# Decoder trunk on one core: the block sums of the seven-product groups on GpSimd instead of VectorE

## The chip, the cores and the metric

The kernel runs on one core of one Trainium2 chip. The metric is the device time of one execution in microseconds, the median of several runs. The core has five engines that work side by side, each through its own queue in order: TensorE (PE in the profile, with PEld for its weight loads) multiplies matrices into PSUM; VectorE (DVE), ScalarE (ACT) and GpSimd (POOL) work elementwise; SyncE (SP) issues nearly all transfers between HBM and SBUF. Semaphores make one engine wait for another.

## The reference, cut to what matters

Two layers, each of three parts with a residual stream `h` of 512 tokens by 1024 features in float32: a feed-forward sub-layer, a mixing sub-layer (three kinds of attention, gated and merged), and a second feed-forward sub-layer.

```
def _swiglu(t, w_gate, w_up, w_down):
    return (jax.nn.silu(t @ w_gate) * (t @ w_up)) @ w_down
...
for l in range(DEPTH):
    f = _swiglu(_rmsnorm(h, ffn1_pre_g[l]), ffn1_w_gate[l], ffn1_w_up[l], ffn1_w_down[l])
    h = h + 0.5 * _rmsnorm(f, ffn1_post_g[l])
    ...
    h = h + _rmsnorm(merged @ w_out[l], mix_post_g[l])
    f = _swiglu(_rmsnorm(h, ffn2_pre_g[l]), ffn2_w_gate[l], ffn2_w_up[l], ffn2_w_down[l])
    h = h + 0.5 * _rmsnorm(f, ffn2_post_g[l])
```

The hidden width of the feed-forward sub-layers is 2816, that is 22 blocks of 128. There are four such sub-layers in all. In the profile their tiles carry the letters `a` (first of a layer) and `c` (second of a layer); `g`, `u` and `d` stand for the gate, up and down weights.

## The kernel before

**Two halves for every operand.** A float32 operand is written as the sum of a high and a low part in a format that TensorE multiplies at full rate. `split` (L179 to L193) makes both: ScalarE casts the high part (L182, `wh_` tiles for weights), VectorE subtracts it from the source (L183, `wl_`; with a scale L185 and L186). A product is then three matmuls (`mm3`, L204 to L208): high by high (L206), high by low (L207), low by high (L208).

**Seven products for eight.** Of the 22 hidden blocks, 16 are computed in two groups of 8 with seven block products in place of eight. Each operand is cut into two by two blocks, and the seven factors are blocks or sums of blocks. On the side of the activations the sums are formed by `sums` (L701 to L733, tiles `x..` and `u..`) and, for the down weights, by `first_factor` (L840 to L858, tiles `as`, `ah`, `al`), all on VectorE. On the side of the weights they are formed by `BlockUnit.load`.

**A weight block.** A `BlockUnit` (L275 to L332) stands for 256 rows by 512 columns of one block, as a tile of 128 partitions by 1024 columns. `fetch` (L301) issues its transfer from SyncE's queue: the block of product `n` goes into a `raw` tile, and for product 2 a second block goes into a kept tile `t` (`tg`, `tu` or `bt` in the profile). `load` (L319) forms what product `n` needs and splits it:

- product 2: `t = t - raw`
- product 3: `t = raw - t`
- product 5: `raw = t - raw`
- product 6: `t = raw - t`
- products 0, 1 and 4: `raw` as it is

These subtractions are line L328. The products come in the order 0, 2, 1, 3, 4, 5, 6, with two units in each; product 2 uses the `raw` tile of product 0 again, product 4 that of product 3. With two groups each of gate, up and down weights there are 8 x 6 = 48 sums in each feed-forward sub-layer, 192 in the kernel. The chain of one block is: transfer, sum where there is one, cast on ScalarE, low part on VectorE, 12 matmuls on TensorE.

**Buffers.** High and low weight tiles have four buffers each, `raw` tiles two, with further room in the `o` tiles while they are free (`BUFS` L102, `RINGS` L349). A block can so be cast at most three units ahead of TensorE, and a transfer starts when a `raw` tile is given back.

**What sets the order.** A queue of jobs (`Queue`, L351 to L462) is walked while the program is written down: each job loads its units, then those of the next jobs (`load_ahead`), then yields its matmuls; `PLAN` (L1668 to L1674) says in which order gate, up and down products of a sub-layer follow one another. The framework then orders each engine's instructions by when it expects their inputs and buffers. `tc.keep_in_program_order` pins an instruction behind what was written down before it on its engine. L329 and L330 pin a sum while the queue is `pinned`, which is so for the units loaded ahead at L646 to L648, and for product 2 of the down weights (`behind`, L907 and L908).

**GpSimd before.** It forms the identity and some constants, issues three small transfers (L122, L123, L156), clears tiles (L1126, L1167, L1217, L1322), and copies rows for the attention (L1215, L1216, L1326, L1390, L1392).

Of the kernel before, what the change touches and what calls it, by code (L numbers as in the profile page):

```python
# [14 lines left out]
ALU = mybir.AluOpType  # L15
# [8 lines left out]
def kernel(  # L24
# [38 lines left out]
    nc = tc.nc  # L63
# [169 lines left out]
    class Unit:  # L233
# [19 lines left out]
        def load(self):  # L253
            if self.h is not None:
                return
            self.fetch()
            self.split_from(self.raw[:])
            self.loaded()
# [16 lines left out]
    class BlockUnit(Unit):  # L275
# [43 lines left out]
        def load(self):  # L319
            if self.h is not None:  # L320
                return
            self.fetch()
            src = raw = self.raw[:]
            if self.n in (2, 3, 5, 6):
                t = self.keep.get(self.k0)
                src = raw if self.n == 5 else t
                a, b = (t, raw) if self.n in (2, 5) else (raw, t)
                ins = nc.vector.tensor_tensor(src, a, b, ALU.subtract)  # L328
                if Q.pinned or self.behind:  # L329
                    tc.keep_in_program_order(ins)  # L330
            self.cast = self.split_from(src)[0]
            self.loaded()  # L332

# [130 lines left out]
    Q = Queue()  # L464
# [1264 lines left out]
```

## Time and profile before

| | us |
|---|---|
| median of 3 runs | 2351.46 (2351.38 to 2351.54) |
| span of the profiled execution | 2349.9 |
| TensorE busy | 2337.9 (99%) |
| VectorE busy | 1799.9 (77%) |
| ScalarE busy | 1506.5 (64%) |
| GpSimd busy | 75.5 (3%) |
| VectorE busy on the sums of L328 | 234.0 (192 instructions) |
| mean DMA rate | 151 GB/s |

The profile comes from one execution, whose span is 1.6 us under the median. Its views give, for a group of instructions with the same line, engine and tiles, the busy time, the mean duration of one, and the idle time of the engine before them with what ended it. The table of stretches gives busy time in a part of the span. In the timeline each row is one instruction, or several alike in a row: start in us, duration in us, engine, line, operation, tiles written and read, shapes, and in brackets the idle time before it and what ended that. Matmuls overlap one another in TensorE, so that their rows are longer than their distance.

### The profile page before, as it was taken

What the parts mean: (1) busy time and instruction counts of PE and PEld (TensorE: products, weight loads), DVE (VectorE), ACT (ScalarE), POOL (GpSimd) and SP (SyncE); (2) the same over time, 40 slices, a digit from 0 to 9 for tenths busy, and PEclk for the clock granted to TensorE, in tenths of its full rate; (3) what the DMA queues carried; (4) which work ended last, traced back from release to release, by engine and by line L of the source; (5) the groups of instructions that cost most, each with busy time, mean ns of one, the idle gap of its engine ahead of it and who ended that gap; (6) DMA issues with size and microseconds to landing.
All of it is one profiled execution on the core that took longest, in us unless ns stands there. A gap on an engine that the chain in (4) does not pass through costs nothing.

```text
span 2349.9 us, 30935 instructions
## 1 busy us (share of the span) xinstructions
PE 2337.9 (99%) x11623; PEld 1977.6 (84%) x11623; DVE 1799.9 (77%) x2359; ACT 1506.5 (64%) x2302; POOL 75.5 (3%) x134
## 2 busy tenths in 40 slices
PE   9999999999999999999999999999999999999998
PEld 7888888888888888888898888888888888888887
DVE  8877877577777688878798788766677766888785
ACT  6677465576766556775656775655777665567744
POOL 0000000000111000000000000000001100000000
PEclk9999999999999999999999999999999999999999
DMA  6667454223323554774646665532323235556744
GB/s 206 186 180 220 149 197 127 81 83 88 90 72 107 189 188 152 198 197 152 226 144 184 204 175 185 182 108 72 100 72 99 73 123 190 171 182 182 217 142 147
DMA packets 297849, 354.96 MB, mean 151 GB/s; under 512 B 78282, under 2 KB 189154, under 8 KB 297700
## 3 DMA queue, kind: packets, MB, share of 16 engines
q1 hardware_dynamic: 297604, 352.97, 49.0%
q8 instruction: 91, 1.49, 0.3%
q14 instruction: 58, 0.48, 0.1%
q0 software_dynamic: 96, 0.03, 0.0%
HBM read 319.39 MB, written 16.78 MB: 143 GB/s over the span
## 4 chain that ended last, share of the span: by engine, by line
PE 89%; DVE 3%; DMA 3%; ACT 3%; issue 2%; SPq 0%; DVEq 0%; ACTq 0%
PE pg L207 3%; PE pg L206 3%; PE pg L208 3%; PE pda L207 3%; PE pdc L207 3%; PE pda L206 3%; PE pda L208 3%; PE pdc L208 3%; PE pdc L206 3%; PE pq L207 1%; PE pq L206 1%; PE pk L207 1%; PE pb L208 1%; PE pk L208 1%; PE pq L208 1%
## 5 line engine op out<-in xcount | busy, mean ns | idle before, releaser
L206 PE MATMUL pg<-us_a,wh_wg 128*128 128x512 f32 x384 | 150.9, 393 | 0.0
L207 PE MATMUL pg<-us_a,wh_wg 128*128 128x512 f32 x384 | 149.7, 390 | 0.0
L208 PE MATMUL pg<-us_a,wl_wg 128*128 128x512 f32 x384 | 149.7, 390 | 0.0
L183 DVE TENSOR_TENSOR wl_da<-raw_da,wh_da 128x1024 fp32r<-128x1024 f32 x50 | 61.0, 1224 | 44.3 <-ACT wh_da L182 44.2
L183 DVE TENSOR_TENSOR wl_dc<-raw_dc,wh_dc 128x1024 fp32r<-128x1024 f32 x50 | 61.0, 1224 | 42.3 <-ACT wh_dc L182 42.3
L207 PE MATMUL pdc<-wl_dc,ahc 128*128 128x512 f32 x224 | 87.7, 391 | 0.0
L207 PE MATMUL pda<-wl_da,aha 128*128 128x512 f32 x224 | 87.6, 391 | 0.0
L208 PE MATMUL pdc<-wh_dc,alc 128*128 128x512 f32 x224 | 87.2, 389 | 0.0
L208 PE MATMUL pda<-wh_da,ala 128*128 128x512 f32 x224 | 87.2, 389 | 0.0
L206 PE MATMUL pdc<-wh_dc,ahc 128*128 128x512 f32 x224 | 86.5, 389 | 0.0
L206 PE MATMUL pda<-wh_da,aha 128*128 128x512 f32 x224 | 86.5, 389 | 0.0
L208 PEld LDWEIGHTS pg<-us_a,wl_wg 128*128 128x128 f32 x384 | 72.1, 188 | 15.1
L207 PEld LDWEIGHTS pg<-us_a,wh_wg 128*128 128x128 f32 x384 | 72.2, 188 | 14.1
L206 PEld LDWEIGHTS pg<-us_a,wh_wg 128*128 128x128 f32 x384 | 72.1, 188 | 14.1
L182 ACT CAST wh_da<-raw_da 128x1024 fp32r<-128x1024 f32 x50 | 52.3, 1051 | 45.6 <-PE pda L208 14.3
L182 ACT CAST wh_dc<-raw_dc 128x1024 fp32r<-128x1024 f32 x50 | 52.3, 1049 | 43.0 <-PE pdc L208 14.1
L186 DVE SCALAR_TENSOR_TENSOR wl_wg<-raw_wg,wh_wg 128x1024 fp32r<-128x1024 f32 x48 | 58.4, 1221 | 21.6 <-ACT wh_wg L185 21.6
L201 DVE SCALAR_TENSOR_TENSOR ga<-pg,bgate,ga 128x512 f32<-128x512 f32 x48 | 35.9, 748 | 48.4 <-ACT ga L200 48.4
L182 ACT CAST wh_uc<-raw_uc 128x1024 fp32r<-128x1024 f32 x44 | 46.3, 1053 | 38.4 <-PE pwc0g L208 9.1
L182 ACT CAST wh_ua<-raw_ua 128x1024 fp32r<-128x1024 f32 x44 | 46.2, 1053 | 31.7 <-PE pwa1g L208 8.6
L185 ACT ACTIVATE wh_wg<-raw_wg 128x1024 fp32r<-128x1024 f32 x48 | 50.6, 1057 | 24.5 <-PE pv L1119 11.7
L183 DVE TENSOR_TENSOR wl_uc<-raw_uc,wh_uc 128x1024 fp32r<-128x1024 f32 x44 | 53.8, 1222 | 16.2 <-ACT wh_uc L182 16.0
(643 smaller groups left out, 8015.9 us busy)
## 6 DMA issues: line engine op xcount, KB each, us to landing
raw_da<-in_ffn_w_down_dram SPq DMA_DIRECT2D x66, 512.0 KB, 4.8
raw_dc<-in_ffn_w_down_dram SPq DMA_DIRECT2D x66, 512.0 KB, 4.3
raw_ga<-in_ffn_w_gate_dram SPq DMA_DIRECT2D x52, 512.0 KB, 4.5
raw_ua<-in_ffn_w_up_dram SPq DMA_DIRECT2D x52, 512.0 KB, 4.5
raw_gc<-in_ffn_w_gate_dram SPq DMA_DIRECT2D x52, 512.0 KB, 4.2
raw_uc<-in_ffn_w_up_dram SPq DMA_DIRECT2D x52, 512.0 KB, 4.0
raw_wg<-in_w_gate_dram SPq DMA_DIRECT2D x48, 512.0 KB, 3.6
raw_wo<-in_w_out_dram SPq DMA_DIRECT2D x24, 512.0 KB, 3.4
```

Source lines behind the costliest of these rows:

```text
L182: both = [nc.scalar.copy(h_ap, src)]
L183: make = lambda: nc.vector.tensor_tensor(l_ap, src, h_ap.bitcast(F32), ALU.subtract)
L185: both = [nc.scalar.activation(h_ap, src, AF.Copy, scale=scale)]
L186: make = lambda: nc.vector.scalar_tensor_tensor(l_ap, src, scale, h_ap.bitcast(F32), ALU.mult, ALU.subtract)
L201: nc.vector.scalar_tensor_tensor(t, z, minus, t, ALU.max, ALU.add)
L206: nc.tensor.matmul(pt, lh, rh, start=start, stop=False, skip_group_check=free)
L207: nc.tensor.matmul(pt, lh, rl, start=False, stop=False, skip_group_check=free)
L208: nc.tensor.matmul(pt, ll, rh, start=False, stop=stop, skip_group_check=free)
```

## The change

The subtraction of L328 is issued on GpSimd in place of VectorE, for every block sum and with the same operands and tiles. The pin of L329 and L330 goes, and nothing pins the sums on GpSimd. Casts, low parts, transfers, buffers and the order of the jobs in the program text stay as they are.

```
@@ -325,9 +325,7 @@
                 t = self.keep.get(self.k0)
                 src = raw if self.n == 5 else t
                 a, b = (t, raw) if self.n in (2, 5) else (raw, t)
-                ins = nc.vector.tensor_tensor(src, a, b, ALU.subtract)
-                if Q.pinned or self.behind:
-                    tc.keep_in_program_order(ins)
+                nc.gpsimd.tensor_tensor(src, a, b, ALU.subtract)
             self.cast = self.split_from(src)[0]
             self.loaded()
```

More of the change, by code (lines that the diff above doesn't have):

```diff
@@ L327, in load @@
                 a, b = (t, raw) if self.n in (2, 5) else (raw, t)
-                ins = nc.vector.tensor_tensor(src, a, b, ALU.subtract)
-                if Q.pinned or self.behind:
-                    tc.keep_in_program_order(ins)
+                nc.gpsimd.tensor_tensor(src, a, b, ALU.subtract)
             self.cast = self.split_from(src)[0]
```

## The prediction

> **What bounds the kernel now.** I read the page first, then the busy time by stretches, then the sums' own line, then pairs of instructions of VectorE and GpSimd that overlap.
>
> ```profile
> span 2349.9 us, 30935 instructions
> PE 2337.9 (99%) x11623; PEld 1977.6 (84%) x11623; DVE 1799.9 (77%) x2359; ACT 1506.5 (64%) x2302; POOL 75.5 (3%) x134
> ```
>
> TensorE (PE) is busy for all but 12.0 us of the span (a stall too short to leave a gap between two matmul rows isn't in this). Where the 12 us lie is in a table of stretches (length, then for PE, weight loads, VectorE, ScalarE and GpSimd the busy us and the number of instructions, then the granted clock, the DMA share and GB/s):
>
> ```profile
> 0.00:30.00 30.00, 27.39 (x162) 21.42 (x163) 19.67 (x46) 18.88 (x34) 3.15 (x9) 1.00 0.89 308
> 30.00:130.00 100.00, 99.56 (x476) 83.53 (x475) 89.37 (x88) 68.58 (x80) 0.00 (x0) 1.00 0.56 160
> ...
> 2210.00:2350.00 140.00, 133.02 (x586) 109.35 (x584) 102.01 (x111) 69.28 (x96) 0.00 (x0) 0.99 0.46 155
> ```
>
> The first 30 us and the last 140 us hold 2.6 + 7.0 = 9.6 of the 12.0 us, before the first sum and mostly behind the last one. Some 2.4 us of visible PE idling is left in the other 2180 us. So nothing that lightens another engine can win more than about 2.4 us, 0.1%. A change can only lose here, by making a weight block late. A measurement of this kernel can tell about 0.2% (4.7 us) from no change.
>
> The edited line is L328. The next fence holds its count and busy time on VectorE over the whole span, then one of its 18 groups by tile (ns min/median/max), then the largest entry of who waited for it (us, times):
>
> ```profile
> 0.00:2350.00 2350.00, 234.00 (x192) 1.00 0.49 151
> L328 DVE TENSOR_TENSOR tga<-raw_ga,tga x16: 1218/1225/1229, 48.1 to 1312.0; 128x1024 f32<-128x1024 f32 x16
>   ACT wh_da L182: 33.3, 12
> ```
>
> 192 sums of 128x1024 float32, 1.22 us each, 48 in each of the four feed-forward sub-layers. ScalarE's cast to the high half of the weights waits for each, VectorE's low half waits for that cast, and TensorE for both.
>
> **What the change removes.** 234 us of VectorE work leave a queue that is idle for almost nothing where it matters: in 50 us at the start of the gate products of each sub-layer (length, busy us of VectorE, count, clock, DMA share, GB/s; the first of four stretches and the sum of the four, then L328 alone in each of them, last the sum of eight longer stretches that hold the other 145 sums):
>
> ```profile
> 30.00:80.00 50.00, 49.93 (x50) 1.00 0.46 146
> ...
> sum 200.00, DVE 198.38; mean DVE 49.59
> 30.00:80.00 50.00, 13.20 (x11) 1.00 0.46 146
> 860.00:910.00 50.00, 12.22 (x10) 1.00 0.47 153
> 1200.00:1250.00 50.00, 15.59 (x13) 1.00 0.39 124
> 2030.00:2080.00 50.00, 14.62 (x13) 1.00 0.52 169
> sum 790.00, DVE 642.74; mean DVE 80.34
> ```
>
> VectorE is idle for 1.6 of 200 us where 47 sums lie, and for 147.3 of 790 us (8 stretches between 80 and 2300 us) where 145 lie. In full stretches a sum takes VectorE less than its duration, since consecutive ones overlap: two take 2.36 us, so the second adds 1.14.
>
> ```profile
> 48.09 2.36 DVE L328 TENSOR_TENSOR tga<-raw_ga,tga 128x1024 f32<-128x1024 f32 x2
> 140.71 1.23 DVE L328 TENSOR_TENSOR tga<-raw_ga,tga 128x1024 f32<-128x1024 f32 x1 [1.13 <-DMA raw_ga<-in_ffn_w_gate_dram]
> ```
>
> The second row is the other thing removed: there VectorE waited 1.13 us for a transfer with its low halves queued behind the sum. On GpSimd that wait holds nobody but later sums.
>
> **What it adds.** 192 two-input instructions on GpSimd, whose queue has no work at all in such stretches (0.00 (x0) in the row of 30 to 130 us). So the ordering pins that the diff drops cost nothing. What a sum can come to stand behind are the few memsets and DMA issues of the stages around, above all these two of the first sub-layer:
>
> ```profile
> 206.76 0.63 POOL L1167 MEMSET cut<- 128x640 f32 x1 [181.86 <-ACT hra L816]
> ...
> 218.59 0.55 POOL L123 DMA_DIRECT2D vecs<-in_b_gate_dram  x1
> ```
>
> The memset stood waiting for 182 us, so a sum queued behind it would be held; but it ran at 206.8 us, when the up products were over, and the two issues of 0.55 us each are read by nothing urgent. I cost these at nothing; if a sum of the down products stands behind both issues, at 1.1 us, once. No row shows a two-input instruction on GpSimd. The nearest are its one-input casts, with as many columns, and with half as many:
>
> ```profile
> L1390 POOL CAST k<-k 64x1024 fp32r<-64x1024 f32 x16 | 16.6, 1036 | 512.0 <-DVE k L183 506.9 <-issue 4.9
> L1216 POOL CAST qk<-k 64x512 fp32r<-64x512 f32 x16 | 9.8, 614 | 0.0
> ```
>
> The slope is (1036 - 614) / 512 = 0.82 ns a column, the fixed part 0.19 us. Low bound: the second input is free, 1.04 us. High bound: two reads and a write each cost a pass of 1024 columns, 0.19 + 3 x 0.84 = 2.7 us. I take 2.07 us, two whole casts, near the middle.
>
> The Trainium skill, GPSIMD Engine Reference, section Performance versus the Vector engine, puts a two-input elementwise operation at 2.6 cycles of 1.2 GHz per column. By that page of the Trainium skill a sum takes about 2.3 us, an estimate that no run here shows, and the forecast below would come out some 11 us later.
>
> **What the two engines do to each other.** This decides the case. Three encounters; first GpSimd reading while VectorE's instruction has two SBUF inputs:
>
> ```profile
> 712.49 1.06 POOL L1392 CAST k<-k 64x512 fp32r<-64x512 f32 x1 [5.12 <-ACT k L182]
> 714.47 0.61 POOL L1392 CAST k<-k 64x512 fp32r<-64x512 f32 x1 [0.92 <-ACT k L182]
> 711.85 1.23 DVE L186 SCALAR_TENSOR_TENSOR wl_wg<-raw_wg,wh_wg 128x1024 fp32r<-128x1024 f32 x1 [0.46 <-ACT wh_wg L185]
> ```
>
> The same cast takes 0.61 us alone and 1.06 us when it begins inside a low-half subtraction: that ends at 713.08, the cast at 713.55, 0.47 us later. The other way round:
>
> ```profile
> 638.42 0.62 POOL L1216 CAST qk<-k 64x512 fp32r<-64x512 f32 x1
> 638.71 0.88 DVE L183 TENSOR_TENSOR o<-ss,o 64x512 fp32r<-64x512 f32 x1
> 1838.21 0.69 DVE L183 TENSOR_TENSOR o<-sf,o 64x512 fp32r<-64x512 f32 x1
> ```
>
> VectorE takes 0.88 instead of 0.69 us; the cast ended at 639.04, 0.33 us after VectorE began. So whoever begins second stands still until the first ends, less about 0.14 us of its own start. With an input in PSUM there is no such thing; here the VectorE instruction keeps its 0.69 us inside a GpSimd cast:
>
> ```profile
> 421.12 1.03 POOL L1390 CAST k<-k 64x1024 fp32r<-64x1024 f32 x1 [201.98 <-DVE k L183]
> 421.63 0.69 DVE L183 TENSOR_TENSOR k<-pk,k 64x512 fp32r<-64x512 f32 x1 [0.65 <-ACT k L182]
> ```
>
> The Trainium skill, SBUF — State Buffer, section Who interferes with whom, has an exclusive lock here: an instruction of VectorE with two SBUF inputs and one of GpSimd that reads SBUF can't run together, and the second fully blocks. The trace agrees in kind (0.61 to 1.06 us), but 0.14 us of the second one's start is hidden; by that page of the Trainium skill each sum would be 0.14 us dearer and the forecast some 6 us later.
>
> The low halves, the sums of the activations and most else of VectorE in these stretches have two SBUF inputs. So a sum on GpSimd doesn't free VectorE: it holds VectorE for 2.07 - 0.14 = 1.93 us instead of 1.14. A sum costs 0.79 us more than before.
>
> **The sum.** In the four full stretches: 47 x 0.79 = 37.1 us, less 1.6 us of idle time. What covers the rest is the lead of the weights over TensorE. Three leads, each a VectorE row and the first matmul that reads what it made:
>
> ```profile
> 63.98 1.23 DVE L183 TENSOR_TENSOR wl_ga<-raw_ga,wh_ga 128x1024 fp32r<-128x1024 f32 x1
> 69.27 0.39 PE L207 MATMUL pwa0g<-wl_ga,uha 128*128 128x512 f32 x1
> 59.44 1.23 DVE L183 TENSOR_TENSOR ula<-x11a,uha 128x1024 fp32r<-128x1024 f32 x1
> 61.11 0.39 PE L207 MATMUL pwa0g<-wl_ga,uha 128*128 128x512 f32 x1
> 61.34 0.39 PE L208 MATMUL pwa0g<-wh_ga,ula 128*128 128x512 f32 x1
> 270.78 1.22 DVE L183 TENSOR_TENSOR wl_da<-raw_da,wh_da 128x1024 fp32r<-128x1024 f32 x1
> 272.05 0.50 PE L207 MATMUL pda<-wl_da,aha 128*128 128x512 f32 x1
> ```
>
> The leads are 4.1, 0.7 and 0.05 us. I take 4.5 us of cover for each full stretch: 37.1 - 1.6 - 18 = 17.5, say 18 us lost. In the eight longer stretches 145 x 0.79 = 115 us stand against 147.3 us of idle time, which hides them on the average, and the token products lose nothing there, since the waits for transfers leave VectorE's queue. But in the down products a weight block arrives with the third kind of lead, twice in each sub-layer: two sums just ahead of it add 1.6 us, of which I let 1.2 show, since VectorE has some idle time there too; 8 x 1.2 = 10 us. Together 28 us. The profiled span of 2349.9 us lies 1.6 us under the median of 2351.5, so: 2349.9 + 28 + 1.6 = 2379.5, say 2380 us.
>
> The ends: with 1.04 us a sum holds VectorE for 0.90 us, less than now, and nothing is lost or, by the bound above, up to 2.4 us won. With 2.7 us the surplus is 1.42 us: 47 x 1.42 - 1.6 - 18 = 47 us, 145 x 1.42 - 147 = 59 us, and with the 10 us 116 us, 2467 us.
>
> **The rivals.**
> *Nothing changes (2351 us).* On GpSimd a sum starts as soon as its block has landed, ahead of its old place in VectorE's queue, and meets VectorE where it is idle or reads PSUM. The place that decides is again the four full stretches: the leads of 18 us and 1.6 us of idle time swallow 47 sums as long as one costs up to 0.42 us more than before, that is up to 1.70 us on GpSimd. For it: this lies well inside the bounds of 1.04 and 2.7 us, and waits for transfers go away. Against it: two inputs for little more than one and a half times the price of one, and 0.8% of idle time.
>
> *GpSimd becomes the bound, slower still (2408 us).* Where the last product of one weight meets the second one of the next, four sums lie in a row: three times among the gate and up products of a sub-layer; at the end of its down products eight lie in a row, twice four. TensorE needs 48 matmuls for four such blocks, at 0.23 us (61.11 to 61.34 above) 10.9 us. If each sum first waits out a low half of 1.14 us, four take 4 x 3.2 = 12.8 us and come 1.9 us late: 5 x 4 x 1.9 = 38 us, of which the 10 us of the down products are counted already: 2380 + 28 = 2408 us. It decides from a sum of 1.6 us up (4 x 2.74 = 10.9). Against it: the blocks of such a row may have landed long before, and be summed early.
>
> *Faster.* VectorE, with 13% less to do and no exclusion, supplies all blocks earlier: at best 2.4 us, 2349 us, within what can't be told from no change. More would need idle time of TensorE that its rows don't show.
> That the sums stay on VectorE is excluded: the edit names the engine.
>
> **How the numbers follow.** The forecast 0.55, GpSimd as the bound 0.25, nothing changes 0.16, faster by more than the trace lets it 0.04. Forecast and bound both end slower by over 0.2%: 0.80; same 0.16; faster 0.04. The range runs from 2350 us, which takes in the case without change, to 2440 us, past the 2408 of the second case and half way into the upper end of the unknown price. The likeliest sign has its own range, 2360 to 2440 us.
>
> **What would show it.** In the profile after, right: 192 subtractions on GpSimd of about 2.1 us, more where they meet VectorE; VectorE's low halves in the products with durations of 1.22 us alone and up to 3 us beside a sum, so that VectorE's busy time falls far less than by 234 us; TensorE idle for some 40 us in place of 12, at the starts of the gate products and in the down products, with low halves (L183) or ScalarE's casts behind GpSimd as releasers. Wrong: low halves of 1.22 us throughout while GpSimd reads (no exclusion for these), a sum of about 1.1 us, or an idle time of TensorE as before. If TensorE idles in bursts where four sums lie in a row, with ScalarE waiting for L328 on GpSimd, the second rival was right. If the instruction order of VectorE or ScalarE moved so that other blocks come late, away from any sum, my account misses the cause.

## The result and the profile after

| | before | after |
|---|---|---|
| median | 2351.42 us | 2523.23 us (2519.00 to 2528.38, 4 runs) |
| ratio | | 1.0733, 95% interval 1.0718 to 1.0748 |
| span of the profiled execution | 2349.9 us | 2517.3 us (its time 2519.0) |

The change costs 172 us, 7.3%. The forecast was 2380 us, with a range up to 2440: right in sign, and far outside in size.

The page of the changed kernel, its span, its busy times and its chain:

```profile
span 2517.3 us, 31181 instructions
PE 2399.9 (95%) x11623; PEld 2005.3 (80%) x11623; DVE 1858.7 (74%) x2167; ACT 1503.3 (60%) x2302; POOL 653.1 (26%) x326
PE 64%; DVE 13%; DMA 8%; ACT 7%; issue 6%; POOL 2%; SPq 0%; DVEq 0%; ACTq 0%; POOLq 0%
```

TensorE (PE) idles for 2517.3 - 2399.9 = 117 us in place of 12. It is also busy for 62 us more with the same 11623 matmuls. VectorE (DVE) has lost 192 instructions of together 234 us, and yet its busy time has gone up, from 1799.9 to 1858.7 us. So what is left on VectorE takes 1858.7 - (1799.9 - 234.0) = 292.8 us longer: 1.52 us for each sum that was taken from it at 1.22 us.

The sums (L328) over the span, and two of their 18 groups (ns min/median/max):

```profile
0.00:2517.30 2517.30, 579.46 (x192) 0.98 0.46 141
L328 POOL TENSOR_TENSOR tua<-raw_ua,tua x16: 2386/2406/3387, 86.3 to 1449.9; 128x1024 f32<-128x1024 f32 x16
L328 POOL TENSOR_TENSOR raw_uc<-tuc,raw_uc x8: 3256/3266/3276, 960.2 to 2303.4; 128x1024 f32<-128x1024 f32 x8
```

A sum takes 2.39 us alone and some 3.3 us where it meets VectorE; the mean is 579.46 / 192 = 3.02 us. That is two and a half times its time on VectorE, and above the 2.07 us of the forecast. All subtractions of L183 on VectorE, before and after (length, busy, count):

```profile
0.00:2349.90 2349.90, 903.63 (x914) 1.00 0.49 151
```

```profile
0.00:2517.30 2517.30, 1115.26 (x914) 0.98 0.46 141
```

The same 914 instructions take 211.6 us more. What that does at one place, the start of a down product of the first sub-layer, is in the timeline. First before, VectorE's queue and the matmul that waits for it:

```profile
214.00 1.22 DVE L183 TENSOR_TENSOR ala<-asa,aha 128x1024 fp32r<-128x1024 f32 x1
215.26 1.23 DVE L851 TENSOR_TENSOR asa<-asa,hra 128x1024 f32<-128x1024 f32 x1
216.40 1.22 DVE L183 TENSOR_TENSOR wl_da<-raw_da,wh_da 128x1024 fp32r<-128x1024 f32 x1
217.54 1.22 DVE L328 TENSOR_TENSOR bta<-bta,raw_da 128x1024 f32<-128x1024 f32 x1
...
217.67 0.50 PE L207 MATMUL pda<-wl_da,aha 128*128 128x512 f32 x1
```

After, the same instructions (lines past L328 are lower by two), with GpSimd's:

```profile
230.77 1.23 DVE L183 TENSOR_TENSOR ala<-asa,aha 128x1024 fp32r<-128x1024 f32 x1 [0.18 <-PE pda L207]
232.03 3.31 DVE L849 TENSOR_TENSOR asa<-asa,hra 128x1024 f32<-128x1024 f32 x1
235.27 3.36 DVE L183 TENSOR_TENSOR wl_da<-raw_da,wh_da 128x1024 fp32r<-128x1024 f32 x1
...
231.16 6.38 POOL L328 TENSOR_TENSOR bta<-bta,raw_da 128x1024 f32<-128x1024 f32 x2 [7.92 <-DMA raw_da<-in_ffn_w_down_dram]
...
238.68 0.50 PE L207 MATMUL pda<-wl_da,aha 128*128 128x512 f32 x1 [4.09 <-DVE wl_da L183]
```

Before, the sum stood behind the low half that TensorE needed next. After, the first of two sums starts when its block has landed, at 231.16 us, and the two take 6.38 us together. Between them and VectorE's two instructions the turn goes back and forth: VectorE's take 3.31 and 3.36 us in place of 1.23 and 1.22, some 4.2 us more together, and TensorE waits 4.09 us. The sums that run here are needed by a later product.

What TensorE waited for, longest totals first (us, times, longest):

```profile
PE pda L207 <- DVE wl_da L183: 27.6, 15, 4.6
PE pdc L207 <- DVE wl_dc L183: 25.2, 13, 4.8
PE pwc0g L206 <- ACT pwc0g L753: 8.8, 2, 4.7
PE pwc1g L206 <- ACT pwc1g L753: 8.6, 2, 5.0
```

The first two rows are the down products; the next two are ScalarE's copy of the first token product's bank, behind which the second product's first matmul stands. None of these rows names a sum. One such copy is late because VectorE's chain ahead of it is late: four sums in a row on GpSimd (two are shown) hold VectorE's instructions, up to the activations' sum `x00c` that the cast needs.

```profile
910.52 3.26 POOL L328 TENSOR_TENSOR raw_gc<-tgc,raw_gc 128x1024 f32<-128x1024 f32 x1
913.74 3.40 POOL L328 TENSOR_TENSOR tgc<-raw_gc,tgc 128x1024 f32<-128x1024 f32 x1
...
911.55 3.30 DVE L722 TENSOR_TENSOR x11c<-x11c,x00c 128x1024 f32<-128x1024 f32 x1
922.69 1.21 DVE L725 TENSOR_TENSOR x00c<-x00c,x10c 128x1024 f32<-128x1024 f32 x1
...
923.93 1.04 ACT L182 CAST uhc<-x00c 128x1024 fp32r<-128x1024 f32 x1 [5.05 <-DVE x00c L725]
924.88 1.06 ACT L753 COPY pwc0g<-pwc0g 128x512 f32<-128x512 f32 x2
```

The copy stands behind the cast `uhc` in ScalarE's queue, the cast waits for `x00c`, and that comes at 923.9 us.

A second loss shows in the granted clock (third number from the right), in three stretches around the stall of the down product above:

```profile
236.40:239.81 3.41, 1.13 (x5) 0.96 (x6) 3.41 (x3) 0.00 (x0) 1.14 (x1) 1.00 1.06 372
239.81:243.22 3.41, 3.41 (x10) 2.64 (x9) 1.24 (x2) 1.82 (x3) 0.00 (x0) 0.50 0.13 47
243.22:246.64 3.42, 3.42 (x17) 2.77 (x16) 3.42 (x4) 2.29 (x3) 0.00 (x0) 1.00 0.00 0
```

After the stall TensorE's clock is 0.50 for 3.41 us, in which 10 matmuls start in place of 17. The changed kernel has 26 such low stretches of 3.4 to 6.8 us, the kernel before one, at its end.

For the runs below the two losses are told apart by TensorE's rows alone: the distance from the start of each 128x512 matmul to the start of the next, less the usual 0.227 us. What exceeds 0.4 us is counted as a stall, what lies between 0.02 and 0.4 us as a slow matmul. The stalls add up to 2.9 us before and 115.0 after, the slow matmuls to 8.5 and 58.1 us: 112 + 50 = 162 of the 167 us between the two spans. Slow is not the same as half clock: of the 58.1 us after, 44 lie in the stretches at 0.50, the others at full clock; before, none of the 8.5 us does.

### The profile page after: what moved, and what is told of

It reads as the page before. It is cut to its first block, busy times and chain, and to the rows that moved or that the text cites. A ratio compares the mean times of both kernels' runs of the same rounds, so it can differ in the third digit from the quotient of the medians.

```text
span 2517.3 us, 31181 instructions
## 1 busy us (share of the span) xinstructions
PE 2399.9 (95%) x11623; PEld 2005.3 (80%) x11623; DVE 1858.7 (74%) x2167; ACT 1503.3 (60%) x2302; POOL 653.1 (26%) x326
## 4 chain that ended last, share of the span: by engine, by line
PE 64%; DVE 13%; DMA 8%; ACT 7%; issue 6%; POOL 2%; SPq 0%; DVEq 0%; ACTq 0%; POOLq 0%
PE pg L207 3%; PE pg L206 3%; PE pg L208 3%; PE pdc L207 2%; DMA raw_da<-in_ffn_w_down_dram 2%; PE pdc L208 2%; PE pda L207 2%; PE pdc L206 2%; PE pda L208 2%; PE pda L206 2%; DMA raw_dc<-in_ffn_w_down_dram 1%; PE pq L207 1%; PE pq L206 1%; PE pk L207 1%; PE pq L208 1%
## 5 line engine op out<-in xcount | busy, mean ns | idle before, releaser
L183 DVE TENSOR_TENSOR wl_dc<-raw_dc,wh_dc 128x1024 fp32r<-128x1024 f32 x50 | 73.0, 1464 | 66.4 <-ACT wh_dc L182 66.4
L207 PE MATMUL pdc<-wl_dc,ahc 128*128 128x512 f32 x224 | 97.3, 435 | 25.2 <-DVE wl_dc L183 25.2
L183 DVE TENSOR_TENSOR wl_da<-raw_da,wh_da 128x1024 fp32r<-128x1024 f32 x50 | 73.9, 1484 | 57.0 <-ACT wh_da L182 57.0
L1388 POOL CAST k<-k 64x1024 fp32r<-64x1024 f32 x16 | 16.6, 1039 | 350.5 <-issue 252.4
L206 PE MATMUL pdc<-wh_dc,ahc 128*128 128x512 f32 x224 | 94.1, 423 | 7.6 <-ACT wh_dc L182 7.6
L183 DVE TENSOR_TENSOR wl_uc<-raw_uc,wh_uc 128x1024 fp32r<-128x1024 f32 x44 | 84.1, 1917 | 23.2 <-ACT wh_uc L182 23.2
L183 DVE TENSOR_TENSOR wl_ua<-raw_ua,wh_ua 128x1024 fp32r<-128x1024 f32 x44 | 78.8, 1799 | 23.5 <-ACT wh_ua L182 23.4
L328 POOL TENSOR_TENSOR tgc<-tgc,raw_gc 128x1024 f32<-128x1024 f32 x8 | 23.1, 2900 | 229.3 <-DMA tgc<-in_ffn_w_gate_dram 115.8
L207 PEld LDWEIGHTS pdc<-wl_dc,ahc 128*128 128x128 f32 x224 | 46.5, 208 | 41.2 <-DVE wl_dc L183 31.2
L183 DVE TENSOR_TENSOR wl_ga<-raw_ga,wh_ga 128x1024 fp32r<-128x1024 f32 x40 | 60.6, 1525 | 25.2 <-ACT wh_ga L182 25.2
```

What stands on the lines that cost most here:

```text
L183: make = lambda: nc.vector.tensor_tensor(l_ap, src, h_ap.bitcast(F32), ALU.subtract)
L206: nc.tensor.matmul(pt, lh, rh, start=start, stop=False, skip_group_check=free)
L207: nc.tensor.matmul(pt, lh, rl, start=False, stop=False, skip_group_check=free)
L328: nc.gpsimd.tensor_tensor(src, a, b, ALU.subtract)
L1388: nc.gpsimd.tensor_copy(t[ro, j::2], t[r, j::2])
```

## The experiments

Three theories. **Exclusion:** a sum on GpSimd and an instruction of VectorE with two SBUF inputs don't run together, so that sums hold the low halves. **Latency:** a sum takes 1.2 us longer on the way from transfer to low half, which would hurt on any engine. **Order:** the framework orders ScalarE's, VectorE's and SyncE's instructions by when it expects their inputs, and the two kernels' orders differ; TensorE's chain is cut by that, not by the sums. Beside each run stands its loss against the kernel before, as measured with it on the same chip (2349.9 to 2350.2 us there).

### Pins, and which sums

The first run leaves the sums on VectorE and drops only their pins:

```
-                if Q.pinned or self.behind:
-                    tc.keep_in_program_order(ins)
```

> The sums stay on VectorE; only the rule that pins some of them to program order goes. Exclusion (GpSimd's sums and VectorE's two-input instructions can't run together) and latency (a sum takes 2.4 us instead of 1.2 on the way from transfer to low half) both expect 2348 to 2358 us, as before. If the lost order of instructions is the cause, a good part of the 172 us shows: over 2400 us.

Measured: 2375.02 us, a ratio of 1.0105 (1.0090 to 1.0120), a loss of 24.9 us. No expectation holds: the theories of the sums had at most 2358 us, that of the order over 2400. On VectorE the pins are worth 25 us. Kept on the GpSimd sums they would change nothing: in the program built that way every engine's instructions stand in the same order.

The next two move the sums of one kind of weights, with the framework's own order: those of the down weights, whose names begin with d, and in the other run (with `!=`) those of the gate and up weights:

```
+                if self.name[0] == "d":
+                    nc.gpsimd.tensor_tensor(src, a, b, ALU.subtract)
+                else:
+                    ins = nc.vector.tensor_tensor(src, a, b, ALU.subtract)
...
```

> Only the 64 sums of the down weights go to GpSimd. In the changed kernel some 77 of 112 us of TensorE's waits lie in the down products, and the lower clock follows them: exclusion and latency both expect 77/112 of 172 us, about 118: 2450 to 2485 us. The terms of the forecast gave 10 us for this part: 2361 us. If the order in the gate and up products is the cause, near 2351.

> Only the 128 sums of the gate and up weights go to GpSimd. The rest of the 172 us by place of the waits, about 50: 2390 to 2415 us. The forecast's terms gave 18 us for this part: 2370 us. If the two parts need each other, e2 and e3 together make less than 172.

Measured: 2437.13 us (+87.0) and 2438.21 us (+88.1). Together 175 us, about the whole loss, so that nothing here speaks for two parts that need each other. The split by the waits, 118 to 50, was wrong, and the forecast's 10 and 18 us were further off; the gate and up sums cost as much as the down sums. Per sum, the 64 of the down weights cost twice as much as the 128 others.

### Exclusion against latency and order

The sums are left out, and in their place GpSimd does work of nearly the same length that reads almost nothing:

```
-                nc.gpsimd.tensor_tensor(src, a, b, ALU.subtract)
+                nc.gpsimd.tensor_tensor(src[:, :, 0:8], a[:, :, 0:8], b[:, :, 0:8], ALU.subtract)
+                for _ in range(2):
+                    nc.gpsimd.memset(src, 0.01)
```

> As the changed kernel, but each sum is replaced by a subtraction of 16 columns and two memsets of the tile, some 2.3 us of GpSimd at the same place, with the same waits and nearly the same order on all engines; the sums are left out (the weights of these groups are a constant). GpSimd reads next to nothing. Exclusion: VectorE's low halves go back to 1.22 us, TensorE's waits go, 2350 to 2375 us. Latency, GpSimd as the bound, or the order of instructions: all of them stay, 2480 to 2530 us.

Measured: 2362.33 us, 1.0052 (1.0037 to 1.0067), a loss of 12.2 us. GpSimd's memsets and one group of low halves in this run (busy, mean ns):

```profile
L330 POOL MEMSET bta<- 128x1024 f32 x48 | 45.8, 955 | 2.8
L183 DVE TENSOR_TENSOR wl_da<-raw_da,wh_da 128x1024 fp32r<-128x1024 f32 x50 | 60.9, 1225 | 51.6 <-ACT wh_da L182 51.6
```

Two memsets and the short subtraction (0.22 us) take 0.22 + 2 x 0.955 = 2.1 us, against 2.39 us for a sum alone, and the low halves are back at 1.225 us (1.484 in the changed kernel). So neither the place of the work nor a length of 2.1 us makes the loss; its reading does.

The same in the order of before. For this run and for all that name that order, the other instructions of ScalarE, VectorE and SyncE were tied in the order in which they stand in the kernel before, by dependencies that need no semaphore. TensorE's 11623 matmuls then come in the order of before too.

```
+    for e, ranks in ((nc.scalar, ACT_ORDER), (nc.vector, DVE_ORDER), (nc.sync, SP_ORDER)):
...
+        for p, i in zip(seq, seq[1:]):
+            tc.add_manual_dep(i, p.name, nosync, reason="order")
```

> The run that only writes (a subtraction of 16 columns and two memsets for each sum on GpSimd, sums left out), in the order of the kernel before. If the 12 us that it cost over before came from the order: 2348 to 2354 us. If they came from the later sum (latency): 2360 to 2365 us.

Measured: 2351.15 us, 1.0005 (0.9996 to 1.0015). A latency of 2.1 us costs nothing that can be told; the 12 us were the order. All L183 subtractions take 906.2 us here, as before:

```profile
0.00:2349.30 2349.30, 906.20 (x914) 1.00 0.49 151
```

Then the real sums on GpSimd in the order of before, the changed kernel with that order forced:

> The changed kernel, all sums on GpSimd, with the order of the other instructions of ScalarE, VectorE and SyncE forced to that of the kernel before. Exclusion: still 2490 to 2525 us, at most the 12 to 25 us that the other order costs by itself are given back. If the changed order is what makes the waits: below 2420 us.

Measured: 2467.94 us, 1.0512 (1.0493 to 1.0530), a loss of 117.8 us. Neither expectation holds: exclusion had 2490 at the least, order below 2420. This run and the last one differ in the sums alone, in what GpSimd reads and in 0.3 us of a sum's own length: the 2467.94 - 2351.15 = 117 us between them are put down to exclusion. The remaining 2523.23 - 2467.94 = 55 us of the change come with the framework's new order, which without exclusion costs only 12. The L183 subtractions take 1141.62 us here:

```profile
0.00:2463.50 2463.50, 1141.62 (x914) 0.99 0.47 144
```

The first two waits of TensorE are those of the down products, as in the changed kernel:

```profile
PE pda L207 <- DVE wl_da L183: 21.3, 12, 4.1
PE pdc L207 <- DVE wl_dc L183: 18.6, 13, 4.1
```

Which engine's order makes the 55 us was tried by forcing one at a time.

> The changed kernel with ScalarE's order alone forced to that of before. Its longest waits in the token products are for ScalarE's copy of the first product (L753), which in the changed kernel stands behind other copies and casts. If ScalarE's order is what makes the 55 us by which the changed kernel exceeds the same one in the order of before: about 2468 to 2480 us. If it is VectorE's or SyncE's: near 2523 us.

> The changed kernel with VectorE's order alone forced to that of before. If VectorE's order makes the 55 us: 2468 to 2480 us; if ScalarE's or SyncE's: near 2523 us.

> The changed kernel with the order of SyncE's transfers alone forced to that of before. If the transfers' order makes the 55 us: 2468 to 2480 us; if not: near 2523 us.

Measured: 2499.60, 2487.61 and 2510.65 us, that is 24, 36 and 13 us less than the changed kernel. The second varies most, from 2481 to 2500 us. No single one makes the 55 us; each gives back a part, and the parts add up to 73 us, more than all three together. With one engine's order forced, the framework's order of the others moves too, so that they are not independent. More than that isn't settled.

Exclusion without a late sum: in the order of before, VectorE makes 16 columns of each sum at once, and GpSimd reads beside it with nobody waiting. The full sums are left out.

```
...
+                beside = nc.gpsimd.tensor_tensor(scr[:], wide, wide, ALU.subtract)
+                tc.add_manual_dep(beside.ins, ins.ins.name, mybir.DependencyInfo(
+                    mybir.DependencyClass.Sync, mybir.DependencyReason.DATA), reason="beside")
```

> The order of ScalarE, VectorE, SyncE and TensorE is that of before. VectorE makes of each sum only 16 columns, at once, so no cast waits for GpSimd; GpSimd runs beside it, after each of them, a subtraction of 1024 columns of a constant into a scratch tile that nobody waits for. The sums are left out. Exclusion by itself, if it needs no late sum: VectorE's low halves still become longer than 1.22 us and most of the 172 us shows, 2450 to 2520 us. If exclusion costs only where a sum is also waited for: 2355 to 2400 us. Latency alone, or the order: 2340 to 2352 us.

Measured: 2390.62 us, 1.0173 (1.0158 to 1.0188), a loss of 40.4 us, at the upper end of the second case. The L183 subtractions take 1032.4 us:

```profile
0.00:2391.00 2391.00, 1032.40 (x914) 0.99 0.48 148
```

That is 129 us more than before for 40 us of loss. So an instruction that nobody waits for slows an engine on the way to TensorE, and the case that the number fits, a cost only where a sum is waited for, isn't what the rows show. Three things keep the cost under 117 us, and the run doesn't tell them apart: GpSimd starts behind the short sum, in the sum's old place in VectorE's queue, not when the block lands; no cast waits for it; and the short sums take VectorE 113.9 us in place of 234.0.

### How the loss grows with the reading

Two sizes in the order of before. Half of the columns summed, the other half filled by a memset (the second halves of the sums are left out):

```
+                c, d = slice(0, 256), slice(256, 512)
+                nc.gpsimd.tensor_tensor(src[:, :, c], a[:, :, c], b[:, :, c], ALU.subtract)
+                nc.gpsimd.memset(src[:, :, d], 0.01)
```

> Order of before; each sum on GpSimd covers only half of the columns, some 1.2 us, and a memset fills the other half, so the second halves of the sums are left out. The forecast's sum: such a sum holds VectorE for 1.06 us, less than the 1.14 us of before, and nothing is lost: 2348 to 2356 us. If the loss follows the time in which GpSimd reads: half of 118 us, about 2410 us. If it is a matter of how long a single low half is held: less than half, 2360 to 2395 us.

And the whole sum in four instructions of 256 columns:

```
+                for k in range(self.nk):
+                    for c in (slice(0, 256), slice(256, 512)):
+                        nc.gpsimd.tensor_tensor(src[:, k, c], a[:, k, c], b[:, k, c], ALU.subtract)
```

> Order of before; each sum on GpSimd is made in four instructions of 256 columns, some 0.75 us each, 3.0 us together. If the length of a single hold decides, a low half waits 0.6 us in place of up to 2.2 us: 2370 to 2430 us. If the whole time in which GpSimd reads decides: 2468 us or more, to 2500 us.

Measured: 2357.72 us (1.0031, 1.0019 to 1.0043, +7.8) and 2511.05 us (+161.1). The rows of GpSimd, first the half sums, then the quarters:

```profile
L329 POOL TENSOR_TENSOR tga<-raw_ga,tga x16: 1282/1296/2277, 35.9 to 1312.6; 128x512 f32<-128x512 f32 x16
```

```profile
L330 POOL TENSOR_TENSOR tua<-raw_ua,tua x64: 722/740/1729, 88.1 to 1453.5; 128x256 f32<-128x256 f32 x64
L330 POOL TENSOR_TENSOR btc<-btc,raw_dc x32: 722/1304/1722, 1110.1 to 2375.9; 128x256 f32<-128x256 f32 x32
```

A reading time of 1.29 us costs 8 us, one of 2.39 us costs 118: half the time brings 7% of the loss. 2357.72 us lies between the ranges that were expected. The forecast's terms had said that a sum which holds VectorE for no longer than before loses nothing (to 2356 us), and that is nearly so. The quarters take 4 x 0.74 = 2.96 us alone, and more where each has to wait for VectorE again. They hold VectorE less in one go, but now the sum itself is late. ScalarE's casts wait for the sum (us, times, longest):

```profile
ACT wh_dc L182 <- POOL btc L330: 66.2, 16, 10.5
ACT wh_da L182 <- POOL bta L330: 63.6, 16, 10.4
```

So neither theory holds. The number lies above the range of the one that counts the whole reading time (to 2500 us), and the reason is another one: shorter turns move the wait from VectorE to GpSimd.

### The two terms of the forecast, each by itself

As the two runs with one kind of sums each, in the order of before.

> Order of before; only the sums of the down weights are on GpSimd. By the waits of the run with all sums in this order (46 of some 70 us in the down products): 46/70 of 118 us, about 78: 2420 to 2435 us. By the forecast's term for this part, 10 us: 2361 us.

> Order of before; only the sums of the gate and up weights are on GpSimd. By the same waits, the rest of 118 us, about 40: 2380 to 2400 us. By the forecast's term for this part, 18 us: 2370 us.

Measured: 2415.99 us (+66.1) and 2400.38 us (+50.5), together 116.6 against 117.8 us with all sums. Both lie just outside the ranges taken from the waits, and far above the forecast's terms. Of the 66 us of the down sums, TensorE's rows show 46 us as stalls and 19 us as slow matmuls; of the 50 us of the others 32 and 10 us. The stalls of the down run are mostly two rows:

```profile
PE pdc L207 <- DVE wl_dc L183: 18.5, 12, 3.9
PE pda L207 <- DVE wl_da L183: 18.4, 13, 3.5
```

25 waits of 1.5 us on the average, about six in each sub-layer. In front of 23 of them, 35.9 of the 36.9 us, a sum ran on GpSimd within the last 5 us before the low half ended that in the kernel before began only behind the same low half.

The matmuls come in the same order in both runs and in the kernel before, so that the start of each can be compared. With the down sums, TensorE falls behind by 62 us in the four stretches of the down products (210 to 300 us, and the three like it). With the gate and up sums it falls behind by 13 us in the four full stretches of 50 us, by 22 us in the eight longer ones, and by 14 us in the time before and between them.

### What a stall of TensorE costs beside itself

In the kernel before, with its order, matmuls of the token products were made to wait for 1 to 8 memsets on GpSimd that start when an earlier matmul is done, at 32 places, 8 of which have two such waits: 40 in all. Nothing is left out.

```
+            one = nc.gpsimd.memset(scr[:], 0.0)
...
+        tc.add_manual_dep(ins.ins, one.ins.name, sync, reason="stall")
```

> The kernel before, with 32 stalls put into the token products: a matmul waits for 1, 2, 3, 4, 6 or 8 memsets of 0.52 us on GpSimd that start when the matmul some 0.7 us earlier is done, or for two stalls of 2 or of 1 memset shortly after each other; 120 memsets, 62 us, with the semaphores some 60 to 70 us. If a stall costs TensorE only itself: 2411 to 2421 us, the granted clock 1.00 throughout. If stalls lower the clock as the low windows of the changed kernel suggest (58 us in windows of half clock beside 115 us of stalls): 25 to 60 us more, 2436 to 2480 us, with clocks of 0.5 for 3.4 us behind the long stalls and none behind the single memsets.

Measured: 2453.39 us, 1.0437 (1.0422 to 1.0453), a loss of 103.2 us. By TensorE's rows the stalls add up to 78.6 us more than before, above the 60 to 70 expected, and the slow matmuls to 22.4 us more, under the 25 to 60 expected; that the total fell into the second range is in part luck. Of the slow matmuls' time, 20 us lie at half clock. The clock by the length of a stall: of 24 stalls of 0.85 or 1.45 us (the doubles are two each) none lowered it; of those of 2.0 us two of four did, of 2.6 us two of four, of 3.8 us three of four, of 4.9 us all four. Whether a stall of 2 us does it depends on where it falls. All low stretches of this run begin on one grid of 3.413 us. Two stalls of 2.0 us, with three stretches of that grid for each (length, busy, count, clock):

```profile
969.65:973.06 3.41, 1.55 (x8) 1.00 1.29 207
973.06:976.47 3.41, 3.41 (x10) 0.50 0.61 120
976.47:979.89 3.42, 3.42 (x17) 1.00 0.81 292
1328.04:1331.45 3.41, 1.94 (x9) 1.00 1.11 309
1331.45:1334.87 3.42, 3.03 (x13) 1.00 0.38 101
1334.87:1338.28 3.41, 3.41 (x17) 1.00 0.96 272
```

The first lies within one stretch, which leaves 1.55 us of busy TensorE in it, and the next one has half the clock. The second is cut by an edge, 1.94 us are left in its first stretch, and the clock stays. The Trainium skill, TensorE: Matmul & The Clock Gate, section What's actually happening, has the grid and the half clock: a free-running window of 3413 ns, and half rate after one idle window. The trace agrees with the grid and with the ratio of 0.50, but the window need not be idle: one with 1.55 of 3.41 us busy was enough. The Trainium skill's advice on the same page, section Why this matters for your kernels, to leave no gaps of over about 3 us, is too mild here: in this run stalls of 1.45 us never lowered the clock, and ones of 2.0 us could.

## Why the prediction was wrong

**What held.** The bound and the sign: TensorE at 99%, with nothing to win. Exclusion: it was read from pairs of one-input casts, and all that it makes costs 117 us, shown by the two runs in the same order that differ in the reading. The forecast has no term for the sum's latency, and at 2.1 us none is needed: 2351.15 us. That VectorE's busy time would fall far less than by 234 us; it rose. The Trainium skill, SBUF — State Buffer, section Who interferes with whom, says that the second of two such instructions fully blocks. The trace agrees: VectorE's instruction beside a sum takes 3.3 us in place of 1.22.

**The step that failed first: each sum at its old place, with 0.79 us more.** The forecast charged the difference, 1.93 instead of 1.14 us, as if the sum still stood in VectorE's queue where it had stood. On GpSimd it starts when its block has landed, and takes the turn ahead of whatever VectorE has next. Before, the sum at 217.54 us came behind the low half that TensorE waited for; after, two sums take their turns in front of it, and TensorE waits 4.09 us. For a low half that is needed at once the price goes up to two whole sums. So the term for the down products was far too small: 8 x 1.2 = 10 us were put down, and 66 us were measured, in some 25 waits instead of 8. That a waiting sum leaves VectorE's queue had been booked as a gain; it is what lets sums run early. Nearly every one of the 25 waits has such a sum in front of it. The early start alone is not enough: the half sums have five such waits of 4.7 us together, and cost 8 us in all. So the changed turn doesn't do it without the length of the sum, and no run tells their shares.

**The size of the sum.** 2.39 us instead of 2.07, inside the bounds of 1.04 to 2.7 us. The estimate from the Trainium skill, GPSIMD Engine Reference, section Performance versus the Vector engine, was 2.3 us, and the trace nearly agrees for a sum alone. With 2.39 us a sum holds VectorE for 2.25 us by the forecast's rule (2.1 us in the rows above), 1.11 more than before, and the forecast's own terms give 47 x 1.11 - 1.6 - 18 = 33 us, 145 x 1.11 - 147 = 14 us and 8 x (2 x 1.11 - 0.4) = 15 us, together 61 us, 2412 us. So the 0.32 us would have been worth 33 us, and 2412 us still misses by 111.

**The cover, too large in the long stretches and too small in the full ones.** With the measured size the first two terms make 47 us, near the 50 us measured for the gate and up sums, but that is luck. The terms put 33 us into the four full stretches, where these sums cost 13; so the lead of the weights covered more than the 4.5 us taken. They put 14 us into the eight longer stretches, for all sums, where the gate and up sums cost 22 us and the down sums 62. The forecast had hidden all of these but 10 us under VectorE's mean idle time, 147 us; that idle time doesn't lie where the waits arise. The time before and between the stretches, 14 us, was not in the sum.

**The order, not in the sum: 55 us.** The forecast said that the dropped pins and the move cost nothing because GpSimd's queue is empty. The order of GpSimd is not the matter. The framework placed ScalarE's, VectorE's and SyncE's instructions anew, and with exclusion this costs 55 us, without it 12. The last sentence of the forecast named such a move as what its account would miss, and gave it no chance.

**The clock, not in the sum.** Stalls of 2 us and more can halve TensorE's clock for the next 3.4 us; 11 of 16 did in the run with stalls alone, which shows it apart from any sum. The slow matmuls at half clock make 44 of the 172 us in the changed kernel, and 26 of the 118 in the order of before; with the gate and up sums alone they make 2 us.

**The rivals.** GpSimd as the bound (2408 us) was wrong as a whole: GpSimd is busy 26%, and TensorE's waits name low halves and copies. Its place, four sums in a row, was one of the places of loss, but what came late at the one shown was VectorE's chain, not the sums. "Nothing changes" decided at 1.70 us a sum; the half sums of 1.29 us bear this out but for 8 us.

**The account.** 117 us exclusion in the order of before (75 in stalls, 33 in slow matmuls; the rest is not split), 1 us latency and 55 us for the order that the framework made of the change. No run was faster than the kernel before. Why the new order loses so much more when GpSimd reads, is open; one place of it, a copy queued behind a late cast, is shown above.

## What to carry to other kernels

Work moved from VectorE to GpSimd frees VectorE only where the two don't exclude each other: look for one overlapping pair of the same operand kinds in the trace, and charge VectorE with the whole duration on GpSimd, at the moment when the inputs land, ahead of the instruction that is most urgent there. This is the price at the worst place; sums of half the length cost next to nothing here. An in-order queue is also a priority: a sum that stood behind the urgent instruction loses that place when it goes to another engine. Where TensorE is the bound, count gaps of about 2 us and more, which may halve the clock, with 1.7 us of lost clock on top for each stretch of 3.4 us at half clock.

## What the runs showed of the hardware beyond what was expected

- A memset on GpSimd beside VectorE's two-input subtractions slows nothing (906.2 against 903.6 us for 914 subtractions); a subtraction there, with nobody waiting, does (1032.4 us).
- Two instructions in turn on each of the two engines alternate: neither gets two turns in a row while the other waits, at the place shown (3.31 and 3.36 us on VectorE beside 6.38 us for two sums).
- TensorE's granted clock can fall to 0.50 for the next 3.41 us when a stall of 2.0 us lies within one stretch of a fixed grid of 3.413 us (two of four such stalls; one that is shown did not when an edge cut it). The 12 stalls of 1.45 us never did it.
